# First layer's norm of a conditioned decoder trunk: scale factors as column products on TensorE, norm times scale in one VectorE pass

## The chip, the cores and the metric

The kernel runs on one core of a Trainium2 chip. The metric is device time in microseconds (us), the median over runs. Engines: TensorE (PE; its weight loads are listed apart as PEld), VectorE (DVE), ScalarE (ACT), GpSimd (POOL); the DMAs are issued by SyncE (SP).

## What is computed

Two layers over 512 positions with width 1024, each a token mixer and a gated feed-forward part, each of the four behind a norm that is modulated by a vector c:

```
cond = silu(c)
for i in range(2):
    mod = cond @ ada_w[i] + ada_b[i]
    sh1, sc1, g1, sh2, sc2, g2 = split(mod, 6)
    h = rms_norm(x, norm_mix[i]) * (1.0 + sc1) + sh1
    mix = stick_breaking_attention(h, ...) if i == 0 else dsa_attention(h, ...)
    x = x + g1 * mix
    h = rms_norm(x, norm_ffn[i]) * (1.0 + sc2) + sh2
    x = x + g2 * conv_ffn(h, ...)

def stick_breaking_attention(h, w_in, w_out):
    q, k, v = split(h @ w_in, 3)      # 16 heads of 64
    z = q k / 8, strictly causal
    a = exp(log_sigmoid(z) + suffix sums of log_sigmoid(-z))
    return (a v) @ w_out
```

The change concerns only the first `h` of layer 0 and what waits for it. The scale sc1 and the shift sh1 are 1024 numbers each, every one a dot product over 1024 elements of `cond`.

## The kernel before

x lies with features on the partitions: 8 tiles (x0 to x7) of 128 features by 512 positions. For accuracy each operand of a projection is split into a high half (rounded by ScalarE, names ending in hi) and the rest (a subtraction on VectorE, names ending in lo); `mm3` then runs three matmuls, hi by hi, lo weights by hi, hi weights by lo (lines 239 to 241). A weight chunk of 128 x 1024 (512 KB) is loaded into a tile `raw`, its halves are `whi` (L199) and `wlo` (L207); `raw` has 6 buffers, `whi` and `wlo` 4 each.

The first stage, in `stick_layer`, is written in a fixed order, and each engine runs its own instructions in that order. Squares of the x tiles on ScalarE (L500) are summed on VectorE; two float32 matmuls with a matrix of 1/1024 (L510, L511) give the mean squares on all partitions; ScalarE makes a seed of the reciprocal root (L514), four VectorE operations refine it to `r` (L516 to L519). GpSimd multiplies each x tile by r (L525, `xr`). In parallel `dots(f)` makes the 128 scales and 128 shifts of feature tile f: a chunk of modulation weights, stored with output features on the partitions, is multiplied on VectorE by `cond` (silu(c), spread over all partitions), and the row sums are accumulated:

```
dve.scalar_tensor_tensor(raw, raw, 1.0, cond, op0=OP.mult, op1=OP.mult, accum_out=dst)
```

That is L248, two per feature tile, and L491 and L494 add the biases and the gain. ScalarE then applies scale and shift (L531, `u`), rounds (`hhi`, L532), and VectorE subtracts (`hlo`, L535). For each feature tile `first_part(i, f)` adds three matmuls to each of four first projections (`pt_first`: q and k of head pairs 0 and 1), 12 per tile and 96 in all. The last two tiles' matmuls stand after the loop, mixed with the next steps.

From there a list of things to do later (`later`, `tick`) sets the order on the other engines: it has a clock of its own that is moved on by hand, and whatever is due is emitted at a `tick`. In the loop over the four projections the halves of the next weight chunks (`split_hi`, `split_lo`) and the evacuations (`evac_q`, `evac_k`, which write `qs`, `kd` and `kz`) are put on it. Then come the first scores z (L680 to L682), which need `qs`, `kd` and `kz`, and behind them on TensorE the value projection `pt_v` and the rest of the layer, which fills TensorE's time between the scores of one head and the next.

Of the kernel before, what the change touches and what calls it, by code (L numbers as in the profile page):

```python
# [18 lines left out]
D = 1024  # L19
# [20 lines left out]
FETCH = 1  # L40
IDXFILL = [1, 1, 1, 0, 1, 1, 1, 1]
# [74 lines left out]
def kernel_body(ctx, tc, xT, wst, cst, smalls, crow, relb, onehot, outT):  # L116
# [29 lines left out]
    cond = condp.enter_context(tc.tile_pool(name="condp", bufs=1)).tile([P, D], F32, name="cond")  # L146
# [22 lines left out]
    def chunk_raw(key, n=D):  # L169
        raw = raws.tile([P, D], F32, name="raw")  # L170
        nc.sync.dma_start(raw[:, :n], wst[CH[key], :, :n])
        return raw
# [17 lines left out]
    def split_hi():  # L190
        i = pos["i"]
        if i >= len(order):
            return
        fetch(i + FETCH)
        k = order[i]
        n = width(k)
        raw = fetched.pop(k)
        hi = splits.tile([P, D], F32R, name="whi")
        act.activation(hi[:, :n], raw[:, :n], AF.Copy)  # L199
        pend_lo.append((k, n, raw, hi))  # L200
        pos["i"] += 1

    def split_lo():
        while pend_lo:
            k, n, raw, hi = pend_lo.pop(0)
            lo = splits.tile([P, D], F32R, name="wlo")
            dve.tensor_sub(lo[:, :n], raw[:, :n], hi[:, :n].bitcast(F32))  # L207
            ready[k] = (hi, lo)

# [36 lines left out]
    def ada_dot(dst, raw):  # L246

        dve.scalar_tensor_tensor(raw, raw, 1.0, cond, op0=OP.mult, op1=OP.mult, accum_out=dst)  # L248
# [214 lines left out]
    def stick_layer(l):  # L463
        with ExitStack() as st:
# [7 lines left out]
            ada_raw = {}  # L472
            for f in range(KT):
                nc.sync.dma_start(x[f], xT[f])
                if f == 3:
                    ada_raw = {g: chunk_raw(("ada", l, g, 0)) for g in (1, 0)}
            fetch(3)
            warm(AF.Silu)
            pc = [ptile([P, S], "pt_c", "tr") for _ in range(2)]
# [5 lines left out]
            gain = sm[:, l * S_L + S_NM:l * S_L + S_NM + KT]  # L485
            dve.scalar_tensor_tensor(sfac, sm[:, sc_b], 1.0, gain, op0=OP.add, op1=OP.mult)
            def dots(f):
                for g in (1, 0):
                    rw = chunk_raw(("ada", l, g, f)) if f else ada_raw[g]
                    ada_dot(mod[l][:, g * KT + f:g * KT + f + 1], rw)  # L490
                dve.scalar_tensor_tensor(sfac[:, f:f + 1], mod[l][:, KT + f:KT + f + 1], gain[:, f:f + 1],  # L491
                                         sfac[:, f:f + 1], op0=OP.mult, op1=OP.add)
                sh = mod[l][:, f:f + 1]
                dve.tensor_add(sh, sh, sm[:, l * S_L + S_ADAB + f:l * S_L + S_ADAB + f + 1])  # L494
# [13 lines left out]
            dots(0)  # L508
# [3 lines left out]
            prefetch(0)  # L512
# [5 lines left out]
            dve.tensor_scalar(t, t, -0.5, 1.5, op0=OP.mult, op1=OP.add)  # L518
            dve.tensor_mul(r, t, r)  # L519
            xr = []  # L520
            raw = {}

            def scaled(f):
                xr.append(ap.tile([P, S], F32, name="xr", tag="ohi" if f < 6 else "qs0", bufs=6 if f < 6 else 2))
                pool.tensor_mul(xr[f], x[f], r)  # L525

            us_ = {}

            def hi_part(f):
                us_[f] = ap.tile([P, S], F32, name="u", tag="olo", bufs=6)  # L530
                act.activation(us_[f], xr[f], AF.Identity, scale=sfac[:, f:f + 1], bias=mod[l][:, f:f + 1])  # L531
                act.activation(hs[f][0], us_[f], AF.Copy)  # L532

            def lo_part(f):
                dve.tensor_sub(hs[f][1], us_.pop(f), hs[f][0].bitcast(F32))  # L535

            for i in range(1, 4):
                scaled(2 * i - 2)
                scaled(2 * i - 1)
                prefetch(i)  # L540
            keys = [("q", 0), ("k", 0), ("q", 1), ("k", 1)]
            cs = [chunk(k, 0) for k in keys]
            pts = [ptile([P, S], "pt_first", "mm" if i < 3 else "x") for i in range(4)]

            def first_part(i, k):
                w = slice(k * P, (k + 1) * P)
                mm3(pts[i], cs[i][0][:, w], cs[i][1][:, w], hs[k][0], hs[k][1], k == 0, k == KT - 1)

            for f in range(KT):
                if f:  # L550
                    dots(f)
                hi_part(f)
                if f < 2:
                    scaled(6 + f)
                if f:
                    lo_part(f - 1)
                    if f < KT - 1:
                        for i in range(4):
                            first_part(i, f - 1)
            lo_part(KT - 1)  # L560
# [186 lines left out]
            for i in range(4):  # L747
                first_part(i, KT - 2)
# [5 lines left out]
                tick(1.3)  # L754
# [542 lines left out]
def _pack(i):  # L1297
    f = {n: np.asarray(v) for n, v in i.items()}
    buf = np.zeros((len(CH), P, D), np.float32)
    for l in range(DEPTH):  # L1300
        b = CH["ada", l, 0, 0]
        buf[b:b + 6 * KT] = f["ada_w"][l].T.reshape(6 * KT, P, D)
    w = f["sb_w_in"][0]
# [41 lines left out]
    for l in range(DEPTH):  # L1345
# [27 lines left out]
        "crow": f["c"][0].reshape(1, D),  # L1373
        "relb": np.ascontiguousarray(f["rel_bias"]),
# [16 lines left out]
```

## Time and profile before

| | |
|---|---|
| median of 3 runs | 1339.51 us (1339.32 to 1339.68) |
| the profiled execution | 1340.01 us, of which span 1338.2 us |
| PE busy | 1287.5 us, 96% of the span |
| DVE busy | 960.8 us, 72% |
| ACT busy | 592.1 us, 44% |
| POOL busy | 23.0 us, 2% |
| mean granted clock of TensorE | 0.992 of full speed |
| chain that ended last | PE 89%, DVE 7%, ACT 2%, issue 1%, DMA 1% |

Times in the trace count from the start of the span. A row of the timeline tells start, duration, engine, line of the kernel, operation, what is written from what, shapes, how many such instructions were merged, and in square brackets how long the engine stood idle before it and what ended that. A matmul's duration includes the time its results take through the array, so matmuls overlap: their pace is the distance between starts. The granted clock is a share of the full 2.4 GHz; 0.5 is the lower level, 1.2 GHz. A float32 matmul is two instructions on the chip.

### The profile page before, as it was taken

To read this page: it belongs to the slowest core of one execution; us is meant where nothing else is said; L and a number is where in the kernel's file an instruction comes from. 1 tells how busy PE (TensorE), PEld (TensorE's weight loads), DVE (VectorE), ACT (ScalarE), POOL (GpSimd) and SP (SyncE) were. 2 spreads that over 40 slices of the span, in tenths; PEclk is the share of its full clock that TensorE was granted. 3 is DMA by queue.
4 is the path that set the end of the run, shared out by engine and by line. 5 is a ranking of instruction groups with operands and counts; after the bars stand their busy time and mean duration, and the time that the engine had idled before them with its cause. 6 is when DMAs were issued, how large, how long until landed. Compare 5 with 4: busy or idle time off the path is not lost.

```text
span 1338.2 us, 17868 instructions
## 1 busy us (share of the span) xinstructions
PE 1287.5 (96%) x6900; PEld 1067.7 (80%) x6900; DVE 960.8 (72%) x1570; ACT 592.1 (44%) x1051; POOL 23.0 (2%) x22
## 2 busy tenths in 40 slices
PE   2899999999999999999999999999999999999998
PEld 0687878799888888888988877766998888888888
DVE  6987988877877877875779986685676546546653
ACT  4575666455323323442554345573454324324430
POOL 3100000000000000000100000000000000000000
PEclk8999999999999999999999999999999999999999
DMA  8724344423575565654212211212222332333221
GB/s 277 239 81 159 122 146 125 143 64 111 174 240 191 182 235 189 191 182 146 79 48 79 79 48 64 56 49 102 79 80 87 103 110 72 111 101 95 72 87 63
DMA packets 49894, 162.68 MB, mean 122 GB/s; under 512 B 5601, under 2 KB 7905, under 8 KB 49810
## 3 DMA queue, kind: packets, MB, share of 16 engines
q1 hardware_dynamic: 49810, 161.55, 37.3%
q8 instruction: 54, 0.88, 0.3%
q14 instruction: 30, 0.25, 0.0%
HBM read 159.39 MB, written 2.14 MB: 121 GB/s over the span
## 4 chain that ended last, share of the span: by engine, by line
PE 89%; DVE 7%; ACT 2%; issue 1%; DMA 1%; SPq 0%; DVEq 0%; ACTq 0%
PE pt_u L240 11%; PE pt_u L239 11%; PE pt_u L241 11%; PE pt_d L241 5%; PE pt_d L239 5%; PE pt_d L240 5%; PE pt_q L239 2%; PE pt_q L241 2%; PE pt_q L240 2%; PE pt_l L239 2%; PE pt_l L240 2%; PE pt_l L241 2%; PE pt_first L241 2%; PE pt_first L239 2%; PE pt_qk L239 2%; PE pt_first L240 2%
## 5 line engine op out<-in xcount | busy, mean ns | idle before, releaser
L199 ACT ACTIVATE whi<-raw 128x1024 fp32r<-128x1024 f32 (+1 forms) x206 | 205.0, 1002 | 146.7 <-PE pt_d L241 106.9
L207 DVE TENSOR_TENSOR wlo<-raw,whi 128x1024 fp32r<-128x1024 f32 (+1 forms) x206 | 240.1, 1168 | 17.0 <-ACT whi L199 15.9
L239 PE MATMUL pt_u<-hhi,whi 128*128 128x512 f32 x640 | 249.4, 390 | 0.0
L241 PE MATMUL pt_u<-hlo,whi 128*128 128x512 f32 x640 | 249.3, 390 | 0.0
L240 PE MATMUL pt_u<-hhi,wlo 128*128 128x512 f32 x640 | 249.3, 389 | 0.0
L806 ACT ACTIVATE y<-pt_u,sm 128x512 f32<-128x512 f32 x80 | 61.9, 774 | 191.6 <-PE pt_u L241 191.6
L239 PEld LDWEIGHTS pt_u<-hhi,whi 128*128 128x128 f32 x640 | 120.2, 188 | 24.9
L241 PEld LDWEIGHTS pt_u<-hlo,whi 128*128 128x128 f32 x640 | 120.2, 188 | 24.9
L240 PEld LDWEIGHTS pt_u<-hhi,wlo 128*128 128x128 f32 x640 | 120.2, 188 | 24.8
L807 DVE SCALAR_TENSOR_TENSOR y<-pt_u,sm,y 128x511 f32<-128x511 f32 x80 | 59.9, 749 | 98.4 <-ACT y L806 98.4
L248 DVE SCALAR_TENSOR_TENSOR raw<-raw,cond 128x1024 f32<-128x1024 f32 x96 | 120.0, 1261 | 0.0
L239 PE MATMUL pt_d<-acthi,whi 128*128 128x512 f32 x288 | 113.9, 396 | 0.0
L241 PE MATMUL pt_d<-actlo,whi 128*128 128x512 f32 x288 | 113.9, 395 | 0.0
L240 PE MATMUL pt_d<-acthi,wlo 128*128 128x512 f32 x288 | 113.8, 395 | 0.0
L350 DVE SCALAR_TENSOR_TENSOR x<-pt_d,mod,x 128x512 f32<-128x512 f32 x48 | 36.0, 750 | 78.6 <-PE pt_d L241 78.6
L239 PE MATMUL pt_first<-hhi,whi 128*128 128x256 f32 (+1 forms) x224 | 69.5, 310 | 7.7 <-ACT hhi L532 7.7
L241 PE MATMUL pt_first<-hlo,whi 128*128 128x256 f32 (+1 forms) x224 | 68.8, 307 | 8.2 <-DVE hlo L535 7.9
L223 ACT ACTIVATE acthi<-y 128x512 fp32r<-128x512 f32 x44 | 27.8, 632 | 104.2 <-DVE y L825 104.2
L240 PE MATMUL pt_first<-hhi,wlo 128*128 128x256 f32 (+1 forms) x224 | 67.9, 303 | 0.0
L241 PEld LDWEIGHTS pt_d<-actlo,whi 128*128 128x128 f32 x288 | 54.1, 188 | 13.2
L240 PEld LDWEIGHTS pt_d<-acthi,wlo 128*128 128x128 f32 x288 | 54.1, 188 | 13.1
L239 PEld LDWEIGHTS pt_d<-acthi,whi 128*128 128x128 f32 x288 | 54.1, 188 | 13.1
(228 smaller groups left out, 2642.5 us busy)
## 6 DMA issues: line engine op xcount, KB each, us to landing
raw<-wst SPq DMA_DIRECT2D x255, 512.0 KB, 3.7
raw<-wst SPq DMA_DIRECT2D x48, 384.0 KB, 3.0
th<-rb SPq DMA_DIRECT2D x16, 256.0 KB, 3.2
x<-xT SPq DMA_DIRECT2D x8, 256.0 KB, 4.6
outT<-x SPq DMA_DIRECT2D x16, 128.0 KB, 1.7
sm<-smalls SPq DMA_DIRECT2D x1, 241.0 KB, 2.5
cons<-cst SPq DMA_DIRECT2D x1, 192.0 KB, 5.1
oh<-onehot SPq DMA_DIRECT2D x1, 80.0 KB, 1.8
```

The costliest lines, as they stand in the source:

```text
L199: act.activation(hi[:, :n], raw[:, :n], AF.Copy)
L207: dve.tensor_sub(lo[:, :n], raw[:, :n], hi[:, :n].bitcast(F32))
L223: act.activation(hi, src, AF.Copy)
L239: pe.matmul(out, lhsT=whi, rhs=ahi, start=start, stop=False)
L240: pe.matmul(out, lhsT=wlo, rhs=ahi, start=False, stop=False)
L241: pe.matmul(out, lhsT=whi, rhs=alo, start=False, stop=stop)
L248: dve.scalar_tensor_tensor(raw, raw, 1.0, cond, op0=OP.mult, op1=OP.mult, accum_out=dst)
L350: dve.scalar_tensor_tensor(x[f][:, c], pt, mod[l][:, g * KT + f:g * KT + f + 1], x[f][:, c], op0=OP.mult, op1=OP.add)
L806: act.activation(y, pt, AF.Identity, scale=cw[2], bias=sm[:, b + S_CB + c:b + S_CB + c + 1])
L807: dve.scalar_tensor_tensor(y[:, 1:], pt[:, :S - 1], cw[1], y[:, 1:], op0=OP.mult, op1=OP.add)
```

## The change

- The scales of all eight feature tiles and the shifts of tiles 0 and 1 are made on TensorE: the modulation chunk, now stored with input features on the partitions, is the weight operand in eight blocks of 128 x 128, and one column of silu(c) is what streams, accumulated over the eight blocks into one column of a PSUM tile `pt_m`. The shifts of tiles 2 to 7 stay row products on VectorE.
- The factor -0.5 of the last refinement step of r goes into the gain (`ghalf`), so that the step takes three VectorE operations instead of four.
- x times r times scale is one VectorE operation that writes `u`; ScalarE adds the shift and rounds in one operation (`hhi`); `hlo` is (u + shift) - hhi on VectorE. GpSimd's products are gone.
- Modulation chunks get buffers of their own (`ada`, six, in space that the attention uses later) and are loaded after x instead of between x3 and x4; the load for tile f + 3 follows the use of tile f. A small DMA (`ccol`, 128 x 8) brings c as a column.
- The order is written anew: the weight halves are made one chunk at a time between the first tiles, and only the last tile's matmuls stay for the loop behind the norm, in which each `tick` is 0.7 instead of 1.3.

```diff
+DVE_SHIFT = range(2, KT)
...
+    def prefetch_now(i):
+
+        while pos["i"] <= i:
+            split_hi(0)
+            split_lo()
...
-            ada_raw = {}
             for f in range(KT):
                 nc.sync.dma_start(x[f], xT[f])
                 if f == 3:
-                    ada_raw = {g: chunk_raw(("ada", l, g, 0)) for g in (1, 0)}
+                    nc.sync.dma_start(cond[:, D:D + KT], ccol)
+            ada_raw = {}
+
+            def load_ada(f):
+
+                for g in (1, 0):
+                    t = ap.tile([P, LW], F32, name="ada", tag="a" if g else "at", bufs=2) if f % 3 < 2 else \
+                        ap.tile([P, QT, 256], F32, name="ada", tag="vs", bufs=2).rearrange("p a b -> p (a b)")
+                    ada_raw[g, f] = t[:, :D]
+                    nc.sync.dma_start(ada_raw[g, f], wst[CH["ada", l, g, f]])
+
+            fetch(0)
+            load_ada(0)
+            fetch(1)
+            load_ada(1)
             fetch(3)
+            load_ada(2)
             warm(AF.Silu)
+            condc = cond[:, D + KT:]
+            act.activation(condc, cond[:, D:D + KT], AF.Silu)
...
             def dots(f):
-                for g in (1, 0):
-                    rw = chunk_raw(("ada", l, g, f)) if f else ada_raw[g]
-                    ada_dot(mod[l][:, g * KT + f:g * KT + f + 1], rw)
-                dve.scalar_tensor_tensor(sfac[:, f:f + 1], mod[l][:, KT + f:KT + f + 1], gain[:, f:f + 1],
-                                         sfac[:, f:f + 1], op0=OP.mult, op1=OP.add)
+
+                by_row = f in DVE_SHIFT
+                pm = ptile([P, 2], "pt_m", "tr")
+                for g in (1,) if by_row else (1, 0):
+                    for k in range(KT):
+                        pe.matmul(pm[:, g:g + 1], lhsT=ada_raw[g, f][:, k * P:(k + 1) * P], rhs=condc[:, k:k + 1],
+                                  start=k == 0, stop=k == KT - 1)
                 sh = mod[l][:, f:f + 1]
-                dve.tensor_add(sh, sh, sm[:, l * S_L + S_ADAB + f:l * S_L + S_ADAB + f + 1])
+                bias = sm[:, l * S_L + S_ADAB + f:l * S_L + S_ADAB + f + 1]
+                if by_row:
+                    ada_dot(sh, ada_raw[0, f])
+                    dve.tensor_add(sh, sh, bias)
+                dve.scalar_tensor_tensor(sfac[:, f:f + 1], pm[:, 1:2], ghalf[:, f:f + 1], sfac[:, f:f + 1],
+                                         op0=OP.mult, op1=OP.add)
+                if not by_row:
+                    dve.tensor_add(sh, pm[:, 0:1], bias)
+                if f + 3 < KT:
+                    load_ada(f + 3)
...
-            dve.tensor_scalar(t, t, -0.5, 1.5, op0=OP.mult, op1=OP.add)
-            dve.tensor_mul(r, t, r)
...
+            dve.scalar_tensor_tensor(r, t, 3.0, r, op0=OP.subtract, op1=OP.mult)
...
             def hi_part(f):
-                us_[f] = ap.tile([P, S], F32, name="u", tag="olo", bufs=6)
-                act.activation(us_[f], xr[f], AF.Identity, scale=sfac[:, f:f + 1], bias=mod[l][:, f:f + 1])
-                act.activation(hs[f][0], us_[f], AF.Copy)
+                us_[f] = ap.tile([P, S], F32, name="u", tag="ohi", bufs=6)
+                dve.scalar_tensor_tensor(us_[f], r, sfac[:, f:f + 1], x[f], op0=OP.mult, op1=OP.mult)
+                act.activation(hs[f][0], us_[f], AF.Identity, bias=mod[l][:, f:f + 1])
...
+            dots(0)
+            hi_part(0)
+            lo_part(0)
+            prefetch_now(1)
+            dots(1)
+            first_part(0, 0)
+            first_part(1, 0)
+            hi_part(1)
+            lo_part(1)
+            prefetch_now(2)
+            first_part(0, 1)
+            first_part(1, 1)
+            dots(2)
+            hi_part(2)
+            prefetch_now(3)
+            lo_part(2)
+            for k in range(2):
+                for i in (2, 3):
+                    first_part(i, k)
+            for f in range(3, KT):
+                dots(f)
                 hi_part(f)
...
+                lo_part(f)
+                if f == 4:
+                    fetch(5)
+                for i in range(4):
+                    first_part(i, f - 1)
...
             for i in range(4):
-                first_part(i, KT - 2)
                 first_part(i, KT - 1)
...
-                tick(1.3)
+                tick(0.7)
```

Three places show the new order. TensorE at the norm; before, the first projections follow the norm's two matmuls:

```order
L510 MATMUL pt_norm<-acc,ones_mean 128x512
L511 MATMUL pt_norm<-sq,ones_mean 128x512
L239 MATMUL pt_first<-hhi,whi 128x512
L240 MATMUL pt_first<-hhi,wlo 128x512
L241 MATMUL pt_first<-hlo,whi 128x512
```

And now:

```order
L545 MATMUL pt_norm<-acc,ones_mean 128x512
L546 MATMUL pt_norm<-sq,ones_mean 128x512
L518 MATMUL pt_m<-cond,ada 128x1 x32
L246 MATMUL pt_first<-hhi,whi 128x512
...
L248 MATMUL pt_first<-hlo,whi 128x512
L518 MATMUL pt_m<-cond,ada 128x1 x8
L246 MATMUL pt_first<-hhi,whi 128x512
```

32 products of tiles 0 and 1 stand between the norm and the first projections; 8 more stand ahead of each later tile's work (12 matmuls of `pt_first` are between such sets).

VectorE's work for one feature tile in the middle of the stage, before:

```order
L248 SCALAR_TENSOR_TENSOR raw,mod_91<-raw,cond 128x1024 x2
L491 SCALAR_TENSOR_TENSOR sfac<-mod_91,sm,sfac 128x1
L494 TENSOR_TENSOR mod_91<-mod_91,sm 128x1
L535 TENSOR_TENSOR hlo<-u,hhi 128x512
L248 SCALAR_TENSOR_TENSOR raw,mod_91<-raw,cond 128x1024 x2
```

And now:

```order
L255 SCALAR_TENSOR_TENSOR ada,mod_91<-ada,cond 128x1024
L524 TENSOR_TENSOR mod_91<-mod_91,sm 128x1
L525 SCALAR_TENSOR_TENSOR sfac<-pt_m,ghalf,sfac 128x1
L558 SCALAR_TENSOR_TENSOR u<-r,sfac,x_98 128x512
L562 SCALAR_TENSOR_TENSOR hlo<-u,mod_91,hhi 128x512
L255 SCALAR_TENSOR_TENSOR ada,mod_91<-ada,cond 128x1024
```

One row product of two is gone, `u` has come from ScalarE, and `hlo` is that of the same tile, right behind its `u`; before it was that of the tile before.

VectorE behind the norm, from the last tile's `hlo` to the scores of the first head (`m` is the first of those), before:

```order
L535 TENSOR_TENSOR hlo<-u,hhi 128x512 x2
L562 CAST ident_b<-cons 128x128
L563 CAST strict_b<-cons 128x128
L207 TENSOR_TENSOR wlo<-raw,whi 128x1024
L608 TENSOR_TENSOR qs_418<-pt_first,qs_418 64x512
L608 TENSOR_TENSOR qs_419<-pt_first,qs_419 64x512
L207 TENSOR_TENSOR wlo<-raw,whi 128x1024
L623 TENSOR_TENSOR kz_400<-pt_first,kd_434 64x512
L623 TENSOR_TENSOR kz_401<-pt_first,kd_435 64x512
L207 TENSOR_TENSOR wlo<-raw,whi 128x1024 x2
```

And now, with what each waits for:

```order
L208 TENSOR_TENSOR wlo<-raw,whi 128x1024 [waits DMAHW7_49,Activation_49]
L208 TENSOR_TENSOR wlo<-raw,whi 128x1024 [waits DMAHW0_49,Activation_49]
L649 TENSOR_TENSOR qs_492<-pt_first,qs_492 64x512
L649 TENSOR_TENSOR qs_493<-pt_first,qs_493 64x512
L208 TENSOR_TENSOR wlo<-raw,whi 128x1024 [waits DMAHW2_49,Activation_49]
L664 TENSOR_TENSOR kz_479<-pt_first,kd_503 64x512
L664 TENSOR_TENSOR kz_480<-pt_first,kd_504 64x512
L208 TENSOR_TENSOR wlo<-raw,whi 128x1024 [waits DMAHW3_49,Activation_49]
```

Two low halves of weights instead of one stand ahead of `qs`, and three instead of two ahead of `kz`. ScalarE's order is the same in both: a high half, two copies of `qs`, a high half, four copies of `kd`, two high halves. Behind this place every engine has the same instructions in the same order as before.

## Rows read from the trace of the kernel before

**Rows 1.** By stretch: busy us (count) of PE, PEld, DVE, ACT, POOL; PEclk; DMA; GB/s.

```profile
60.00:70.00 10.00, 7.84 (x58) 7.07 (x58) 8.55 (x12) 9.83 (x18) 0.00 (x0) 1.00 0.64 201
70.00:80.00 10.00, 10.00 (x77) 9.19 (x77) 6.54 (x11) 6.28 (x16) 0.00 (x0) 1.00 0.03 11
```

**Rows 2.** Timeline, VectorE and TensorE between the norm and the first projection's beat.

```profile
21.59 5.63 DVE L207 TENSOR_TENSOR wlo<-raw,whi 128x1024 fp32r<-128x1024 f32 x3
...
27.14 2.28 DVE L248 SCALAR_TENSOR_TENSOR raw<-raw,cond 128x1024 f32<-128x1024 f32 x1
...
34.56 0.80 PE L241 MATMUL pt_first<-hlo,whi 128*128 128x512 f32 x1 [7.86 <-DVE hlo L535]
```

**Rows 3.** Timeline, one beat of the feature tiles, VectorE and TensorE.

```profile
42.78 1.21 DVE L248 SCALAR_TENSOR_TENSOR raw<-raw,cond 128x1024 f32<-128x1024 f32 x1
...
43.95 0.39 PE L239 MATMUL pt_first<-hhi,whi 128*128 128x512 f32 x1
...
44.18 0.39 PE L240 MATMUL pt_first<-hhi,wlo 128*128 128x512 f32 x1
...
45.87 1.22 DVE L248 SCALAR_TENSOR_TENSOR raw<-raw,cond 128x1024 f32<-128x1024 f32 x1
```

**Rows 4.** Timeline, the tail behind the first projection.

```profile
57.52 1.06 ACT L199 ACTIVATE whi<-raw 128x1024 fp32r<-128x1024 f32 x1 [1.31 <-PE pt_first L241]
...
61.31 1.23 DVE L207 TENSOR_TENSOR wlo<-raw,whi 128x1024 fp32r<-128x1024 f32 x1
...
63.09 1.99 ACT L199 ACTIVATE whi<-raw 128x1024 fp32r<-128x1024 f32 x2
63.22 1.41 DVE L623 TENSOR_TENSOR kz<-pt_first,kd 64x512 fp32r<-64x512 f32 x2 [0.68 <-ACT kd L628]
...
64.22 0.37 PE L239 MATMUL pt_v<-whi,hhi 128*128 128x256 f32 x1
...
65.14 0.28 PE L240 MATMUL pt_v<-whi,hlo 128*128 128x256 f32 x1
...
65.26 0.28 PE L241 MATMUL pt_v<-wlo,hhi 128*128 128x256 f32 x1
```

**Rows 5.** Timeline, squares and norm.

```profile
5.58 2.66 ACT L500 ACTIVATE sq<-x 128x512 f32<-128x512 f32 x4 [3.35 <-DMA x<-xT]
...
11.45 1.30 ACT L500 ACTIVATE sq<-x 128x512 f32<-128x512 f32 x2 [2.73 <-DMA x<-xT]
...
14.52 2.08 PE L510 MATMUL pt_norm<-acc,ones_mean 128*128 128x512 f32 x2 [7.73 <-DVE acc L507]
...
18.34 0.69 ACT L514 ACTIVATE r<-pt_norm,eps_c 128x512 f32<-128x512 f32 x1 [1.62 <-PE pt_norm L511]
...
20.52 0.43 DVE L518 TENSOR_SCALAR t<-t 128x512 f32<-128x512 f32 x1
20.98 0.69 DVE L519 TENSOR_TENSOR r<-t,r 128x512 f32<-128x512 f32 x1
```

**Rows 6.** Timeline, one-column matmuls of the second layer (ssq) between long ones.

```profile
717.58 0.39 PE L241 MATMUL pt_q<-hlo,whi 128*128 128x512 f32 x1
717.80 0.95 PE L912 MATMUL ssq<-ones,q 128*128 128x1 f32 x8
...
718.93 0.39 PE L240 MATMUL pt_q<-hhi,wlo 128*128 128x512 f32 x1
```

**Rows 7.** Granted clock in two stretches (as rows 1), and timeline around 797 us.

```profile
22.00:24.00 2.00, 0.00 (x0) 0.00 (x0) 2.00 (x2) 0.04 (x1) 2.00 (x2) 0.61 0.29 78
...
38.00:40.00 2.00, 2.00 (x6) 1.23 (x6) 2.00 (x6) 0.74 (x1) 1.84 (x4) 0.62 0.66 248
...
795.35 0.39 PE L1105 MATMUL z<-kph,qh 128*128 128x256 f32 x1 [1.14 <-DVE L L1116]
...
797.35 0.63 PE L240 MATMUL pt_q<-hhi,wlo 128*128 128x512 f32 x1
797.77 0.63 PE L241 MATMUL pt_q<-hlo,whi 128*128 128x512 f32 x1
```

## What is predicted, and why

> **What bounds the kernel now.** I read the busy times by stretch first. From 70 us on TensorE is busy in the whole of each stretch, and in the 10 us before it is not [rows 1]. So a change of the first stage is worth what it does to the moment at which the value projection (pt_v) starts: all that follows is the same list of instructions, led by TensorE, and moves as one block. In the run before that moment is 64.22 us [rows 4]. Every number below is a shift of it.
>
> The timeline says what leads up to it. After the norm VectorE makes three low halves of weights beside GpSimd's products, at 1.88 us each, and then row products that take 2.28 us, so that the first low half of h comes late: TensorE stood 7.86 us for it and goes on at 34.56 [rows 2]. Then there is a steady beat: a row product of the one feature tile starts at 42.78, that of the next at 45.87, so 3.09 us per tile, and VectorE never rests [rows 3]. TensorE needs less: matmuls of 512 columns start 0.23 us apart there, and 12 of them are 2.75 us. So VectorE bounds this stretch, by 0.34 us per tile.
>
> Then comes a tail. The first projection is complete when ScalarE goes on at 57.52; that moment I call T0. ScalarE then works through weight halves and copies, VectorE makes kz at 63.22, the scores need kz, and pt_v starts 6.70 us after T0, while TensorE mostly stands [rows 4].
>
> **The front, part by part.** Before, two chunks of modulation weights (1 MB) stood ahead of x4 in the DMA queue, and ScalarE waited 2.73 us for x4, until 11.45 [rows 5]. Now x comes first. In exchange a small activation of c's column stands ahead of the first square, and its DMA is queued behind x0 to x3. The fourth square began at about 7.56 (5.58 + 3 x 0.66) without a wait, so x3 had landed by then; the first square now starts between 5.6 and about 7.3. Eight squares and two Silu of 0.6 us on end take 6.5 us, so the last square ends between 12.1 and 13.8, against 14.27 before. I take the late half, and the norm's matmuls start at about 13.5, 1.0 us before the 14.52 of rows 5. They end in r's seed at 18.34 - 1.0 = 17.3. The scale of r loses one operation, 0.46 us from start to start (20.52 to 20.98), so r is ready at 21.67 - 1.0 - 0.46 = 20.2.
>
> **The products on TensorE.** 80 matmuls of one column are added: 16 each for tiles 0 and 1, 8 each for the other six. In float32 each is two instructions on the chip, 160 in all. The trace has the same shape: eight such instructions stand between matmuls of 512 columns that start at 717.58 and 718.93 [rows 6]. Of these 1.35 us two steps of 0.23 are the neighbours' own, so 0.89 us is left for eight, 0.111 each. A set of 8 matmuls (16 instructions) costs 1.78 us, all of them 17.8 us, on the engine that has to run the stage.
>
> The Trainium skill (TensorE: Matmul & The Clock Gate, LDWEIGHTS) puts a load of 128 weight columns at 107 ns, by which 160 would take 17.1 us. Its Back-to-back issue gap gives a matmul of 1 to 64 columns a floor of about 25 ns, by which they would take 4 us if the loads hid; rows 6 have each load beside a matmul that is too short to hide it, and side with the first.
>
> The chain at the higher clock: norm done 17.3; sets of tiles 0 and 1, 64 x 0.111 = 7.1, to 24.4. VectorE has u(0), lo(0) and the second weight half by then (20.9 + 0.4 + 0.7 + 0.8 + 0.7 + 1.2 = 24.7). Six matmuls to 26. Tile 1: shift and scale 24.6, u 25.7, high half 26.4, low half 27.1; six matmuls, waiting 0.8 us in all for it, end at 28.2. Set 2 to 30.0, three matmuls to 30.7; the fourth weight half is queued on VectorE behind u(2), which needs set 2 (30.0 + 0.2 + 0.8 + 1.2 = 32.2), so the next three end at 32.8 and the last six at 34.2. Then five rounds of one set and 12 matmuls, 1.78 + 2.75 = 4.53 us each, to 56.8, and three matmuls: T0 at 57.6. In these rounds VectorE needs 1.3 (row product) + 0.35 + 0.7 (u) + 0.8 (waiting for the high half) + 0.7 = 3.9 us, and lies beside TensorE. So the beat goes from 3.09 to 4.53 us, and the earlier start is eaten: T0 moves by +0.1. What is taken from VectorE and GpSimd is worth nothing more, since TensorE is late next.
>
> DMAs: the six modulation buffers come free in turn, the last pair after set 4 at about 41, needed at 52. Even x4, which had to land behind all that was issued in the first 4 us, was there at 11.45 [rows 5], so 11 us of cover are enough and nothing waits; if that cover went, each late chunk would cost its lateness.
>
> **The tail.** TensorE has only the last tile's 12 matmuls left at T0, and the order of VectorE changes: two low halves before qs, a third before kz. That third one waits for ScalarE's third high half, which stands behind the four copies of kd. In rows 4 that high half starts at 63.09 and two take 1.99, so it ends at 64.1; a low half is 1.23, so kz starts at 65.3 instead of 63.22 at the same T0: +2.1. Queued behind it on VectorE is kz, behind kz on TensorE the scores, and behind these pt_v.
>
> **The clock.** In the run before TensorE stood from 18.3 on, and the granted clock was at its lower level, half, through 38 us: rows 7 have it fall in the stretch 22 to 24 and rise in 38 to 40, after matmuls had run on end from 34.56, so 4.9 us. In the new tail TensorE stands from 59.6 to about 66.2 but for one short matmul, so I expect the clock to be at its lower level (1.2 GHz) when pt_v starts. At 1.2 GHz a matmul of 512 columns starts every 0.42 us [rows 7], so one of 256 every 0.21, against 0.12 [rows 4]; 3.5 to 4.9 us of that lose 1.5 to 2.1. I take +1.8; nothing if the clock holds.
>
> Whether the products hold the higher clock in the front no row shows. From above they cost nothing more. From below: all 64 at twice the pace (7.1 us more), set 2 too (1.8), and 24 matmuls at 0.43 (4.8 more), less what waits hide: about +12. The nearest row is 793 to 797: TensorE did short matmuls on either side of a wait of 1.14 us, and those after it start at the lower pace [rows 7]. I take it that it falls in the products and rises within the first two dozen matmuls: 12 at +0.2 less the 0.8 us of waiting that they hide, and 6 more, +2.8.
>
> **Sum.** 0.1 + 2.1 + 1.8 + 2.8 = +6.8 us. The profiled execution took 1340.01 with a span of 1338.2, so it would be 1346.8; it lies 0.5 over the median of 1339.51, and the forecast for a median is 1346.3.
>
> **Rivals.**
> The clock holds through the products: for it, the weight loads keep TensorE busy in the profile; against it, 793 to 797. Without the 2.8: +4.0, 1343.5. If it held in the tail too, +2.2, 1341.7.
> The products are cheap, and it is not slower: one mechanism, the pace of a one-column instruction in a long run. With pairs at 0.055, half of rows 6, the sets take 8.8 us, VectorE with 3.9 us per round leads, T0 is about 53.7, and pt_v starts at 62.5 plus up to 1.8: -1.7 to +0.1, 1338.5. It decides below 0.086 us (4.0 / 160 = 0.025 less than 0.111). For it: the rows are of eight instructions, not 16 to 64. Against it: all are alike. The Trainium skill's floor of 25 ns (the same page) would be this rival.
> The lower clock lasts, and products slow with it: near the bound of +12 in the front with the tail's 3.9 on top, about 1351.5 in the middle and 1355.5 at the end. For it: sets of one column come again between the dozens. Against: 12 matmuls on end should raise it.
> The change does not do what it says, as VectorE still leads: then its beat of 3.9 us shows, and the time is that of cheap products.
>
> **Chances.** Forecast (+4.8 to +10) 0.50; clock holds (+2.2 to +4.8) 0.23; cheap products 0.17; long low clock 0.10. No change means within 0.2%, 2.7 us, about what can be told apart here. Faster by more needs cheap products and an earlier norm and no clock loss: 0.08. Within: the rest of cheap products and the low end of the second case, 0.15. Slower: 0.77. The range leaves out the fastest of the third case and the slow end of the fourth: 1338.3 to 1352.
>
> **What would show it.** Right: 64 product instructions from about 17 us in some 7 to 9 us; rounds of about 4.5 us after tile 2 with VectorE waiting for pt_m; kz behind a third low half, and pt_v near 69 to 72; a lower clock at its start. Wrong: rounds of 3.9 us or less, T0 before 55.4, or a granted clock of 1.0 from 17 us on.

## The result, and the profile after

The changed kernel takes 1352.87 us (median of 4 runs, 1351.97 to 1357.07) against 1339.55 for the kernel before on the same chip: slower, ratio 1.0103 [1.0092, 1.0115]. The forecast was 1346.3 with a range up to 1352.0: the sign holds, but +6.8 became +13.3, just outside the range.

The profiled execution of the changed kernel is its slowest, 1357.07 us with a span of 1355.3. First the busy time, from the page:

```profile
PE 1314.5 (97%) x7060; PEld 1096.7 (81%) x7060; DVE 949.4 (70%) x1558; ACT 586.6 (43%) x1044; POOL 6.7 (0%) x14
```

TensorE is busy 27 us longer, VectorE 11 us less, and GpSimd's products are gone. By stretch (us busy and count of PE, PEld, DVE, ACT, POOL, then granted clock), the answer to [rows 1]:

```profile
60.00:70.00 10.00, 10.00 (x58) 8.74 (x58) 5.55 (x14) 2.06 (x3) 0.00 (x0) 1.00 0.51 204
70.00:80.00 10.00, 3.53 (x16) 2.87 (x16) 7.71 (x9) 9.58 (x16) 0.00 (x0) 0.83 0.48 149
```

The stretch in which TensorE stands has moved by ten microseconds: it now begins behind 71, where TensorE was busy throughout before. The timeline of TensorE says why; norm and products, the answer to [rows 5]:

```profile
13.82 2.08 PE L545 MATMUL pt_norm<-acc,ones_mean 128*128 128x512 f32 x2 [6.61 <-DVE acc L543]
15.69 1.92 PE L546 MATMUL pt_norm<-sq,ones_mean 128*128 128x512 f32 x2
17.39 13.65 PE L518 MATMUL pt_m<-cond,ada 128*128 128x1 f32 x64
30.91 0.77 PE L246 MATMUL pt_first<-hhi,whi 128*128 128x512 f32 x1
```

The norm begins 0.7 us earlier. Then 64 product instructions take 13.5 us from start to start, 0.211 each, about twice the 0.111 of [rows 6], and the first projection begins at 30.91 where it began at 25.48. Next, ScalarE, VectorE and TensorE after the set of tile 2:

```profile
35.98 1.84 PE L518 MATMUL pt_m<-cond,ada 128*128 128x1 f32 x16
...
38.11 0.75 DVE L558 SCALAR_TENSOR_TENSOR u<-r,sfac,x 128x512 f32<-128x512 f32 x1
...
38.90 0.72 ACT L559 ACTIVATE hhi<-u,mod 128x512 fp32r<-128x512 f32 x1 [5.10 <-DVE u L558]
39.53 1.04 ACT L200 ACTIVATE whi<-raw 128x1024 fp32r<-128x1024 f32 x1
40.60 1.23 DVE L208 TENSOR_TENSOR wlo<-raw,whi 128x1024 fp32r<-128x1024 f32 x1 [1.73 <-ACT whi L200]
40.62 0.80 PE L246 MATMUL pt_first<-hhi,whi 128*128 128x512 f32 x1 [1.98 <-ACT whi L200]
...
41.88 0.80 PE L247 MATMUL pt_first<-hhi,wlo 128*128 128x512 f32 x1 [0.46 <-DVE wlo L208]
```

The set is at 0.11 per instruction again. But the fourth weight chunk's high half stands on ScalarE behind tile 2's `hhi`, which needs that set: TensorE stands 2.44 us. The rounds, with the start of a set in each and VectorE behind it (rows 3 were the beat before):

```profile
54.80 1.84 PE L518 MATMUL pt_m<-cond,ada 128*128 128x1 f32 x16
...
59.35 1.84 PE L518 MATMUL pt_m<-cond,ada 128*128 128x1 f32 x16
...
61.23 0.22 DVE L525 SCALAR_TENSOR_TENSOR sfac<-pt_m,ghalf,sfac 128x1 f32<-128x1 f32 x1 [0.67 <-PE pt_m L518]
```

4.55 us per round (forecast 4.53), and VectorE waits for the set. The tail, the answer to [rows 4]:

```profile
69.39 1.06 ACT L200 ACTIVATE whi<-raw 128x1024 fp32r<-128x1024 f32 x1 [1.84 <-PE pt_first L248]
...
74.95 1.99 ACT L200 ACTIVATE whi<-raw 128x1024 fp32r<-128x1024 f32 x2
76.03 1.23 DVE L208 TENSOR_TENSOR wlo<-raw,whi 128x1024 fp32r<-128x1024 f32 x1 [0.72 <-ACT whi L200]
...
77.28 1.41 DVE L664 TENSOR_TENSOR kz<-pt_first,kd 64x512 fp32r<-64x512 f32 x2
...
78.45 0.56 PE L246 MATMUL pt_v<-whi,hhi 128*128 128x256 f32 x1
...
79.23 0.41 PE L246 MATMUL pt_v<-whi,hhi 128*128 128x256 f32 x1
79.44 0.42 PE L247 MATMUL pt_v<-whi,hlo 128*128 128x256 f32 x1
```

T0 is 69.39, kz stands behind a third low half, and pt_v starts 9.06 us after T0, before 6.70. Its matmuls start 0.21 apart, against 0.12. The clock, as in [rows 7]:

```profile
39.00:45.00 6.00, 3.92 (x8) 2.77 (x9) 3.19 (x5) 1.56 (x2) 0.00 (x0) 0.51 0.30 98
77.00:83.00 6.00, 4.89 (x23) 4.92 (x24) 4.86 (x8) 2.95 (x6) 0.00 (x0) 0.50 0.63 182
```

It is low after the stand at the fourth half and again at pt_v. Behind pt_v every engine's instructions are as before.

### The profile page after: what moved, and what is told of

Read it like the earlier page. It is cut to its first block, busy times and chain, and to the rows that moved or that the text cites. A ratio compares the mean times of both kernels' runs of the same rounds, so it can differ in the third digit from the quotient of the medians.

```text
span 1355.3 us, 18155 instructions
## 1 busy us (share of the span) xinstructions
PE 1314.5 (97%) x7060; PEld 1096.7 (81%) x7060; DVE 949.4 (70%) x1558; ACT 586.6 (43%) x1044; POOL 6.7 (0%) x14
## 4 chain that ended last, share of the span: by engine, by line
PE 92%; DVE 4%; ACT 2%; issue 1%; DMA 1%; SPq 0%; DVEq 0%; ACTq 0%
PE pt_u L247 11%; PE pt_u L246 11%; PE pt_u L248 11%; PE pt_d L248 5%; PE pt_d L247 5%; PE pt_d L246 5%; PE pt_first L246 2%; PE pt_first L247 2%; PE pt_first L248 2%; PE pt_q L246 2%; PE pt_q L248 2%; PE pt_q L247 2%; PE pt_l L246 2%; PE pt_l L247 2%; PE pt_l L248 2%; PE pt_m L518 2%
## 5 line engine op out<-in xcount | busy, mean ns | idle before, releaser
L255 DVE SCALAR_TENSOR_TENSOR raw<-raw,cond 128x1024 f32<-128x1024 f32 x80 | 96.8, 1217 | 0.0
L247 PEld LDWEIGHTS pt_d<-acthi,wlo 128*128 128x128 f32 x288 | 54.0, 188 | 13.5
```

What stands on the lines that cost most here:

```text
L247: pe.matmul(out, lhsT=wlo, rhs=ahi, start=False, stop=False)
L255: dve.scalar_tensor_tensor(raw, raw, 1.0, cond[:, :D], op0=OP.mult, op1=OP.mult, accum_out=dst)
```

## The experiments

In their profiles T0 and pt_v are as the prediction defines them; the "rest" is the span minus the start of pt_v, 1273.98 before and 1276.85 after. Medians of the kernel before in the three groups of runs: 1339.88, 1340.12, 1340.49.

**e1_tick**: the tick of the last loop back to 1.3.

```diff
-                tick(0.7)
+                tick(1.3)
```

> The changed kernel with tick(1.3) in place of tick(0.7) in the loop behind the norm, so that VectorE's order there is again that of the kernel before: one low half of weights ahead of qs and two, not three, ahead of kz. Theory (the tail's new order costs 2.1 to 2.4 us, and the long stand of TensorE ahead of pt_v then starts it at the lower clock for another 2 us): from T0 (ScalarE's high half behind the first projection) to pt_v 6.7 us instead of 9.06; 2 to 5 us less than the changed kernel's 1352.9, so 1348 to 1351. Rival (the order does not matter, since kz waits for ScalarE's copies in any case): 9 us from T0 to pt_v as before, no change of the time.

Measured 1353.93 (1349.72 to 1355.14), ratio 1.010 [1.0085, 1.0116]. In the profile T0 is 65.31:

```profile
70.87 1.99 ACT L200 ACTIVATE whi<-raw 128x1024 fp32r<-128x1024 f32 x2
71.00 1.41 DVE L664 TENSOR_TENSOR kz<-pt_first,kd 64x512 fp32r<-64x512 f32 x2 [0.68 <-ACT kd L669]
...
72.01 0.36 PE L246 MATMUL pt_v<-whi,hhi 128*128 128x256 f32 x1
```

kz now waits for `kd` alone, and T0 to pt_v is 6.70 again: the 2.36 us of the tail are the tick's. The median does not show them and lies above the forecast 1348 to 1351; the runs lie 5 us apart, so nothing can be said of their worth from it. The profiles agree with them: against e11 below, the changed kernel with a front of like length, the span is 2.1 us shorter (1347.7 against 1349.8), although T0 is 0.6 later.

**e2_shift0**: all shifts as row products on VectorE, 64 matmuls instead of 80.

```diff
-DVE_SHIFT = range(2, KT)
+DVE_SHIFT = range(0, KT)
```

> The changed kernel with the shifts of tiles 0 and 1 as row products on VectorE too (DVE_SHIFT = range(0, KT)): 16 matmuls instead of 32 of one column between the norm and the first projections, 64 in all instead of 80. Theory (what is lost in the front is the number of products times 0.21 us per instruction at the lower clock): the burst behind the norm takes 6.7 us instead of 13.6, the first projection's matmuls start at 24 to 26 instead of 30.9, T0 5 to 7 us earlier, time 1345 to 1348. Rival (the front is bound by VectorE and by the weight halves, and the two row products that it gets back cost what the products did): T0 within 2 us of 69.3, time about 1352.

Measured 1356.99 (1353.51 to 1357.65), 1.0123 [1.0108, 1.0139]: not faster. TensorE in its profile:

```profile
17.85 4.00 PE L518 MATMUL pt_m<-cond,ada 128*128 128x1 f32 x32
24.01 0.79 PE L246 MATMUL pt_first<-hhi,whi 128*128 128x512 f32 x1 [2.17 <-ACT hhi L559]
...
36.75 0.80 PE L246 MATMUL pt_first<-hhi,whi 128*128 128x512 f32 x1 [2.00 <-ACT whi L200]
```

The products shrink to 4.0 us, but the row products put `u` and the weight halves later on VectorE, TensorE stands instead, and pt_v is at 74.76. T0 is 65.70, 3.7 us before that of the first profile (5 to 7 were expected) and 1.0 behind that of e11. In the front, the number of instructions on TensorE alone does not give the time.

**e3_warm**: three float32 matmuls of 512 columns of x, used by nothing, ahead of the norm.

```diff
+            busy = ptile([P, S], "pt_busy", "mm")
+            for i in range(3):
+                pe.matmul(busy, lhsT=ones_mean, rhs=x[i], start=True, stop=True)
             warm(AF.Abs_reciprocal_sqrt)
```

> The changed kernel with three matmuls added ahead of the norm (a matrix of 1/1024 times x0, x1, x2, float32, 512 columns, result not used), while TensorE otherwise stands, so that the granted clock is at its higher level when the norm's matmuls and the products begin. Theory (one-column products do not hold the higher clock): the norm's two matmuls take about 1.9 us instead of 3.6, the products start near 15.7 at 0.11 us per instruction, the clock falls within them and the rest run at 0.21; T0 2 to 6 us earlier. Rival (they hold it once it is there): all 64 at 0.11, the first projection's matmuls near 23 and at 0.23 each, T0 8 to 10 us earlier, time about 1343. Second rival (the level does not come from TensorE's own work): nothing changes.

Measured 1352.86 (1349.21 to 1354.79), 1.0096 [1.0078, 1.0113]. TensorE in its profile:

```profile
13.89 1.12 PE L548 MATMUL pt_norm<-acc,ones_mean 128*128 128x512 f32 x2 [1.62 <-DVE acc L543]
...
15.71 10.34 PE L518 MATMUL pt_m<-cond,ada 128*128 128x1 f32 x64
```

And two stretches of it, with the granted clock:

```profile
17.00:19.00 2.00, 2.00 (x20) 2.00 (x20) 1.93 (x4) 0.00 (x0) 0.00 (x0) 1.00 1.03 422
20.00:29.00 9.00, 9.00 (x36) 8.37 (x36) 4.29 (x8) 3.34 (x4) 0.00 (x0) 0.50 0.86 327
```

Norm and first products run at the higher clock, 20 instructions in 2 us; then it falls to 0.50 in the middle of the products, with the PE row busy throughout. So a run of 64 product instructions did not hold the higher clock that it was given. T0 is 63.54, 5.9 us before that of the first profile but only 1.1 before that of e11, and the median is that of the changed kernel.

**e4_one_product**: one block of eight in every product (scales and the shifts of tiles 0 and 1 are not the reference's).

```diff
-                    for k in range(KT):
-                        pe.matmul(pm[:, g:g + 1], lhsT=ada_raw[g, f][:, k * P:(k + 1) * P], rhs=condc[:, k:k + 1],
-                                  start=k == 0, stop=k == KT - 1)
+                    pe.matmul(pm[:, g:g + 1], lhsT=ada_raw[g, f][:, :P], rhs=condc[:, :1], start=True, stop=True)
```

> The changed kernel with one matmul of one column in place of the eight of each product (the scales, and the shifts of tiles 0 and 1, are then made of an eighth of their sum): 10 such matmuls in all, every DMA, wait and order as it was. Theory (the products on TensorE are what costs; beside them the new front is led by VectorE at about 3.9 us per feature tile): first projection from 22 to 23 us on, rounds of 3.9 us, T0 at 52 to 55 instead of 69.3, and with the tail as it is a time of 1337 to 1341. Rival (VectorE or the modulation loads bind the stage as much as TensorE): rounds stay near 4.5 us, T0 at 60 or later, time over 1345.

Measured 1342.0 (1340.98 to 1342.78), 1.0014 [1.0005, 1.0023]. Its front, two rounds on VectorE, and T0:

```profile
21.43 0.80 PE L246 MATMUL pt_first<-hhi,whi 128*128 128x512 f32 x1 [2.83 <-ACT hhi L557]
...
45.42 0.75 DVE L560 SCALAR_TENSOR_TENSOR hlo<-u,mod,hhi 128x512 fp32r<-128x512 f32 x1 [0.79 <-ACT hhi L557]
...
49.21 0.75 DVE L560 SCALAR_TENSOR_TENSOR hlo<-u,mod,hhi 128x512 fp32r<-128x512 f32 x1 [0.79 <-ACT hhi L557]
...
54.40 1.06 ACT L200 ACTIVATE whi<-raw 128x1024 fp32r<-128x1024 f32 x1 [1.43 <-PE pt_first L248]
```

The first projection starts at 21.43, rounds are 3.79 us and led by VectorE, T0 is 54.40, 3.1 us earlier than before; the tail is 9.06 and the clock low at pt_v (63.46). So about 11 of the 13 us are the products, and all else in the change together costs some 2 us: the tail (2.4) and the clock behind it (2.2 of the rest) take back more than the 3.1 gained up to T0.

**e12_front_only**: whole products for tiles 0 and 1, one block for tiles 2 to 7 (whose scales are not the reference's).

```diff
-                    for k in range(KT):
+                    blocks = KT if f < 2 else 1
+                    for k in range(blocks):
...
```

> The changed kernel with whole products for tiles 0 and 1 and one of eight blocks for tiles 2 to 7 (their scales are not what the reference has). It divides the 11 us that all products cost between the front and the rounds. Theory (the front at the lower clock costs most): the first pt_first at 27.5 to 31 instead of 21.4, the rounds at 3.8 us as without products, time 1342.0 plus 6 to 8, 1348 to 1350; the rounds' part is then 3 to 5 us, near 5 x 0.76. Rival (the sets in the rounds cost most, the front is hidden by waits anyway): at most 1345.

Measured 1349.42 (1345.77 to 1350.41), 1.0061 [1.0044, 1.0078]; rounds of 3.8 us on VectorE. The front of its profile, which is its fastest run:

```profile
17.64 10.56 PE L519 MATMUL pt_m<-cond,ada 128*128 128x1 f32 x64
28.06 0.77 PE L246 MATMUL pt_first<-hhi,whi 128*128 128x512 f32 x1
```

The 64 instructions in the front, 8 in e4, cost 7.4 us between the medians, 6.8 when each is taken against its own group's kernel before, as the theory had it; its four runs lie 4.6 us apart, so the figure is rough. The sets in the rounds are the other 3.5 to 4.7 us (to the medians of the changed kernel), about 5 x 0.76.

**e5_order**: e1, and the fourth weight halves ahead of tile 2's products.

```diff
+            prefetch_now(3)
             dots(2)
             hi_part(2)
-            prefetch_now(3)
             lo_part(2)
```

> The changed kernel with tick(1.3) as in the run before, and with the fourth weight half (k of pair 1) made ahead of tile 2's scale instead of behind its high half. Theory (in the changed kernel TensorE stands some 3 us there, since ScalarE makes the weight's high half only behind tile 2's, and VectorE its low half behind that; the clock then falls a second time): no stand between set 2 and the last six matmuls of tiles 0 and 1, T0 4 to 5 us earlier than with tick(1.3) alone in like clock, time 1347 to 1350. Rival (what stands there is hidden by the products and costs only itself): T0 1 to 2 us earlier, time 1352 or more.

Measured 1346.97 (1345.2 to 1350.1), 1.0056 [1.0037, 1.0074]. TensorE does not stand from 27.85 to the tail, the clock stays high from 31.4 on until 65.5, and T0 is 60.59 with the first projection at 27.85, where e1 had 65.31 with it at 27.53. The order of the fourth half thus cost 5 us of T0: some 2.8 of stand (in e1), and most of the rest a second fall of the clock, after which nine matmuls of 512 columns start 0.43 apart.

**e8_tail**: e5, and three unused matmuls (as in e3) behind the last tile.

```diff
+            busy = ptile([P, S], "pt_busy", "z")
+            for i in range(3):
+                pe.matmul(busy, lhsT=ones_mean, rhs=x[i], start=True, stop=True)
             warm(AF.Sigmoid)
```

> As the run with tick(1.3) and the fourth weight half ahead of tile 2's scale, and three float32 matmuls more (result not used) behind the last tile's, where TensorE stands for kz. Theory (pt_v starts at the lower clock because TensorE stands ahead of it): the clock is high at pt_v, its matmuls of 256 columns start every 0.12 us from the first on, time 1.5 to 2.5 us below that run. Rival (the stand is still long enough, or the fall comes from elsewhere): the clock is low at pt_v in this run too, same time.

Measured 1344.92 (1342.96 to 1347.57), 1.0039 [1.0026, 1.0051]. The unused matmuls and pt_v:

```profile
65.87 2.74 PE L797 MATMUL pt_busy<-x,ones_mean 128*128 128x512 f32 x6
...
70.60 0.30 PE L722 MATMUL z<-kz,qs 128*128 128x128 f32 x1 [1.70 <-DVE kz L664]
...
70.77 0.36 PE L246 MATMUL pt_v<-whi,hhi 128*128 128x256 f32 x1
...
71.21 0.28 PE L246 MATMUL pt_v<-whi,hhi 128*128 128x256 f32 x1
71.33 0.28 PE L247 MATMUL pt_v<-whi,hlo 128*128 128x256 f32 x1
```

They lie in time that TensorE spends waiting, pt_v runs 0.12 apart, and the rest is 1274.43, against 1276.45 in e5. In all profiles the rest tells whether the clock was low at pt_v: 1273.98 (before), 1274.43 (e8), 1274.21 (e7), 1274.46 (e10) where not, and 1275.6 to 1276.9 in the ten others. So the lower clock there costs 1.1 to 3.0 us. The medians of e8 and e5 differ by as much as the rest (2.05 and 2.02), but their intervals overlap; the rest is the evidence.

**e6_tile1**: the kernel before, and only tile 1's scales and shifts as column products, behind the norm.

```diff
+BY_COLUMN = (1,)
...
+            for f in BY_COLUMN:
+                products(f)
...
+                if f in BY_COLUMN:
+                    sc, src = pms[f][:, 1:2], pms[f][:, 0:1]
...
```

> The kernel before, with one part of the change: scale and shift of tile 1 alone as column products on TensorE, between the norm and the first projections, where TensorE stands idle in the kernel before. Theory (column products are free only in that idle stretch, and there they take two row products of 2.28 us off VectorE, which leads): products from about 20 to 26 us, first low half near 28 instead of 32.8, T0 and pt_v 4 to 5 us earlier, time 1335 to 1336.5 against 1339.9. Rival (the loads of the two chunks and the products at the lower clock come too late, or VectorE is as long busy with something else): T0 within 1.5 us, no change; or later, and slower.

Measured 1339.44 (1337.35 to 1340.56), 0.9994 [0.9985, 1.0004]: no change. The products take 6.96 us at 19.66, within TensorE's stand but for the last 1.0 us (the first projection begins at 26.48, and then waits for the low half). VectorE is rid of two row products of 2.28 us, yet:

```profile
28.74 2.29 DVE L249 SCALAR_TENSOR_TENSOR raw<-raw,cond 128x1024 f32<-128x1024 f32 x1
...
36.08 2.30 DVE L249 SCALAR_TENSOR_TENSOR raw<-raw,cond 128x1024 f32<-128x1024 f32 x1
...
38.31 1.22 DVE L249 SCALAR_TENSOR_TENSOR raw<-raw,cond 128x1024 f32<-128x1024 f32 x1
```

GpSimd still has the same products to do, and the next row products run beside it at the slow pace until 38. T0 is 54.95, 2.6 us earlier; the clock is low at pt_v (61.82), which takes 1.7 of it.

**e7_onepass**: the kernel before, and only the one VectorE pass.

```diff
-                pool.tensor_mul(xr[f], x[f], r)
...
-                act.activation(us_[f], xr[f], AF.Identity, scale=sfac[:, f:f + 1], bias=mod[l][:, f:f + 1])
-                act.activation(hs[f][0], us_[f], AF.Copy)
+                dve.scalar_tensor_tensor(us_[f], r, sfac[:, f:f + 1], x[f], op0=OP.mult, op1=OP.mult)
+                act.activation(hs[f][0], us_[f], AF.Identity, bias=mod[l][:, f:f + 1])
...
```

> The kernel before, with another part of the change alone: x times r times scale in one VectorE pass, shift and rounding in one ScalarE operation, and GpSimd's eight products gone; row products, buffers and order as before. Theory (beside GpSimd VectorE is slowed, 1.88 for 1.22 and 2.28 for 1.22; taking GpSimd away gives back about 6 us until 39 us, and the eight passes cost 0.75 each): weight halves and row products at 1.22, first low half near 30, rounds of about 4.3 us per tile instead of 3.09, T0 within 2 us of 57.5 and no clear change of the time (1338 to 1342). Rival (the one pass is a gain by itself, hidden in the changed kernel by the products): T0 5 us earlier, 1335. Second rival (it is a loss, since VectorE leads): T0 5 us later, 1345.

Measured **1337.29** (1335.86 to 1338.52), 0.9979 [0.9970, 0.9989]: ahead of both kernels, and with e9 the fastest. The answer to [rows 2]:

```profile
21.21 3.49 DVE L207 TENSOR_TENSOR wlo<-raw,whi 128x1024 fp32r<-128x1024 f32 x3
24.61 0.74 DVE L524 SCALAR_TENSOR_TENSOR u<-r,sfac,x 128x512 f32<-128x512 f32 x1
25.28 1.22 DVE L248 SCALAR_TENSOR_TENSOR raw<-raw,cond 128x1024 f32<-128x1024 f32 x1
...
28.48 0.75 DVE L528 SCALAR_TENSOR_TENSOR hlo<-u,mod,hhi 128x512 fp32r<-128x512 f32 x1
```

Without GpSimd beside it three low halves take 3.49 us instead of 5.63, and a row product 1.22 instead of 2.28. The beat rises from 3.09 to 3.87 us, but the first low half begins at 28.48 instead of 32.75; T0 is 53.98, 3.5 us earlier, and pt_v (60.69) runs 0.12 apart, at the higher clock. The time lies between the theory's (no clear change) and the rival's 1335. The Trainium skill (GPSIMD Engine Reference, Specifications) says that GpSimd shares its memory interfaces with VectorE, with contention for VectorE's instructions that have two inputs in that memory; the trace agrees, 1.22 against 2.28.

**e9_one_t1** and **e10_one_t12**: e7 with the column products of e6 for tile 1, and for tiles 1 and 2. From e9 to e10:

```diff
-BY_COLUMN = (1,)
+BY_COLUMN = (1, 2)
```

> The kernel before with x times r times scale in one VectorE operation (no GpSimd products), and with the scales and shifts of tile 1 alone made as column products on TensorE, behind the norm's two matmuls, where TensorE stood 8.2 us in the run with the one pass alone. Theory (products are free where TensorE stands anyway and cost their whole time where it does not): 32 product instructions at 0.21 us, 7 us, fit into that stand; VectorE loses two row products of 1.15 us, so the first projection ends 2.3 us earlier than with the one pass alone (53.98 to about 51.7), pt_v starts near 58.4, and the time is about 1335.0. Rival (the lower clock at pt_v eats what is gained, as with tile 1 alone): pt_v near 58.4, but the clock falls there and 1.7 us are lost again, 1336.7. Second rival (any product costs its time): 1338 or more.

> As the run before it in this group, with the column products of tiles 1 and 2 on TensorE behind the norm. Theory: 64 instructions at 0.21 us are 13.5 us, 5 us more than the stand holds, so the first projections start at 31 to 32 instead of 26.2 with many matmuls due at once; VectorE, 4.6 us lighter, no longer leads. First projections from 31.5: 96 at 0.23 is 22 us, with 2.5 to 5 us for the lower clock, so T0 at 57 to 59 and the time 1338 to 1341, 3 to 5 us over the run with tile 1 alone. Rival (VectorE's load decides): another 2.3 us earlier, about 1333.

Measured 1337.5 (1335.99 to 1338.08), 0.9976 [0.9966, 0.9987], and 1338.94 (1337.19 to 1341.48), 0.9991 [0.9982, 1.0001]. With tile 1 the products (20.11 to 25.69) hide in TensorE's stand, T0 is 52.41 and pt_v starts at 59.12, 1.6 us earlier than in e7; the clock falls at 60.0, the rest is 1275.98, and nothing is left: the first rival of that expectation. With two tiles the products take 13.8 us, the first projection starts at 33.01 and T0 is 55.73, 1.75 later than in e7: the time is where the theory had it (1338 to 1341), but only 1.4 over e9 instead of 3 to 5, and T0 is earlier than its 57 to 59.

**e11_changed_again**: the changed kernel, unaltered.

> The changed kernel once more, unaltered, to see how far its own executions lie apart. Theory: the time depends on where in the front the clock rises and falls, so the median is again about 1353 within a spread of some 5 us, and a profile with the first pt_first earlier than 30.9 has a shorter span by about as much. Rival (its spread is the chip's own and the first value stands): all within 1352 to 1354, with the same front.

Measured 1354.13 (1351.48 to 1361.93), 1.012 [1.0083, 1.0157]. The profiled execution took 1351.58, 5.5 us less than the first one, and its front differs; TensorE, and then two stretches with the granted clock:

```profile
13.26 2.08 PE L545 MATMUL pt_norm<-acc,ones_mean 128*128 128x512 f32 x2 [6.31 <-DVE acc L543]
...
16.83 10.54 PE L518 MATMUL pt_m<-cond,ada 128*128 128x1 f32 x64
27.23 0.77 PE L246 MATMUL pt_first<-hhi,whi 128*128 128x512 f32 x1
```

The stretches:

```profile
17.00:19.00 2.00, 2.00 (x21) 2.00 (x19) 1.17 (x2) 0.69 (x1) 0.00 (x0) 1.00 1.03 420
21.00:29.00 8.00, 8.00 (x34) 7.70 (x35) 3.57 (x6) 2.22 (x3) 0.00 (x0) 0.50 0.75 257
```

Here the clock rose before the products, 21 instructions ran in 2 us, and then it fell, as in e3. In the first profile all 64 went at the low pace. The same kernel thus has two fronts 3.7 us apart.

## Why the prediction was off

The shift of the end against the kernel before: up to pt_v in three parts, and what lies behind pt_v (us):

| part | forecast | first profile | e11 |
|---|---|---|---|
| start of the first projection (before 25.48) | -1.1 | +5.4 | +1.8 |
| from there to T0 (before 32.04) | +4.0 | +6.4 | +5.4 |
| T0 to pt_v (before 6.70) | +2.1 | +2.4 | +2.4 |
| behind pt_v | +1.8 | +2.9 | +2.1 |
| sum | +6.8 | +17.1 | +11.6 |

- **The norm 1.0 us earlier**: 0.7 and 1.3, counted in the first row. About right, though the first square started at 7.91, later than the 5.6 to 7.3 that were given.
- **The term that failed is the clock in the front, +2.8.** The step read "I take it that it falls in the products and rises within the first two dozen matmuls". It charged the lower clock to 18 matmuls behind the products and to none of the products: the 64 stayed in the chain at 7.1 us, the higher clock's price. They took 13.5 us in the first profile and 10.4 in e11. In the first, all of them went at 0.211 each; in e11 some 20 went at 0.1 and then the clock fell. Entering at the higher clock does not save the price: in e3 the norm's first matmul took 1.12 us, where [rows 5] and the changed kernel have 2.08, and the products still took 10.2. The pace of [rows 6] is that of the higher clock. The forecast's own bound of +12 had all 64 at twice that pace; the choice between the ends was wrong. The front's products, with the 7.1 us that were counted, cost some 7 of the 11 us that all products cost (e12 over e4).
- **A wait was sized too small.** The chain put the fourth weight half behind `u` on VectorE alone, which left TensorE about 1.4 us of waiting (from 30.7 to the matmuls that end at 32.8). Its high half also stands behind `hhi` on ScalarE: 2.4 and 2.8 us in the two profiles, and the clock falls a second time, which the chain did not have (e5 over e1: 5 us of T0 in all).
- **Rounds of 4.53 us, TensorE late next**: 4.55, with VectorE waiting 0.67 us for `pt_m`. Right, so the rival in which VectorE still leads is out; e4 shows VectorE's own rounds at 3.79 (3.9 was said).
- **The tail, +2.1**: +2.36, by the third low half ahead of kz. Right, and e1 undoes it in its profile.
- **The lower clock at pt_v, +1.8**: +2.9 and +2.1, right in kind; e8 takes away the 2.0 that it cost in e5.
- **Rivals.** "The clock holds" and "cheap products" are out; the price of an instruction at the higher clock was right (a set of 16 takes 1.70 us from its start to that of the next matmul, 0.106 each, against 0.111). The Trainium skill (TensorE: Matmul & The Clock Gate, LDWEIGHTS) gives a load of P columns P / 1.2 ns, without a level of the clock, by which 128 columns would take an estimated 107 ns; the traces show 0.106 us per instruction at the higher level and 0.211 at the lower one, so the measurement decides and the rule holds at one level alone. "The lower clock lasts", with 1351.5 to 1355.5, is nearest to what came, with a chance of 0.10: too little, as the nearest row (793 to 797) pointed that way. It is right for the products of the front and wrong for the rounds, whose sets ran at the higher pace; that the time lies in its range is in part luck, since the longer wait for the fourth weight half is in it too.

The times of the changed kernel lie 5 to 10 us apart, those of the kernel before within 4. The two forms of the front go with that as far as profiles can tell: six of them have this front, and the products take 10.5 us in four (e1, e5, e11, e12) and 13.65 in two (the first, e8). When the norm starts does not decide it: at 13.26 to 14.07 us in the four, at 13.25 and 13.82 in the two. The longest execution, 1361.93, lies 5 us beyond both profiles of the changed kernel and has none. What decides when the clock rises in one execution and not in another stays open; no run isolates it.

## What to carry to other kernels

Before work is moved to TensorE, read the clock where it will stand, by the pace of the matmuls already there, price it at that level, and do not take it that the work will hold a higher one. One-column products here ran at the pace of their weight loads, 0.106 or 0.211 us each (in the stretch shown last the loads are busy for 15.37 of 16 us). A run of 64 neither raised the clock nor held it, while sets of 16 between longer matmuls ran at the higher pace. Work moved to an engine that stands anyway can hide (e9's products did, and T0 came 1.6 us earlier), but even there the time did not change, since the clock fell at pt_v. The part worth having was the one pass (e7, 2.8 us). Its rows show VectorE faster with GpSimd gone from beside it; no run takes away GpSimd's products and nothing else, so that they are the whole of the gain is argued, not shown.

## What was not expected of the hardware

- The granted clock fell to 0.50 inside a run of products during which the PE row is busy throughout (e3, e11; 9.00 of 9 us and 8.00 of 8).
- In the stretch of the first profile where products went at 0.211 the clock's column reads 1.00. In e7, e8 and e10 it reads 1.00 through the whole first stage, whose paces change. The pace of the instructions is the better witness there:

```profile
18.00:34.00 16.00, 16.00 (x69) 15.37 (x69) 6.98 (x13) 3.66 (x5) 0.00 (x0) 1.00 0.68 230
```

- The small activation that makes silu(c) as a column (128x8) waited 5.56 us for its DMA (to 7.79), and the first square stood behind it; the norm was nevertheless earlier than before.
